# Gated delta rule: the state-free part of all chunks computed beside convolution and memory projection and kept in DRAM, on one Trainium2 core

## The chip, the cores and the metric

The kernel runs on one core of a Trainium2 chip. The metric is the device time of one execution in microseconds, the median of several runs. Before the change it is 1636.0 us (three runs, 1629.88 to 1637.38).

## What is computed

One layer of a hybrid decoder trunk on x of 1024 positions by 1024 columns, all float32. Cut to what matters here:

```
h = rms_norm(x);  proj = h @ w_in
qkv, z, a, b, c_q, c_kv, k_idx, w_idx, ug = split(proj)
qkv = silu(causal_depthwise_conv(qkv, 4 taps))     # 4 heads of 128, for q, k and v
q, k = l2_norm(q), l2_norm(k)                      # per head and position
# delta rule in chunks, here of 128 positions, 8 chunks; gamma = decay inside a chunk
A  = strict_lower(beta k k^T * gamma);  qk = lower(q k^T * gamma)
u, w = solve(I + A, [beta v, beta k exp(decay)])
# scan over chunks with a state S (128x128 per head):
v_new = u - w S;  o = (q exp(decay)) S + qk v_new;  S = S exp(last) + k_dec^T v_new
y_a = rms_norm(o) * silu(z)
y_b = attention over the 256 best-scored earlier positions (top-k) of 4 heads of 64
y_c = silu(layer_norm(causal_depthwise_conv(u * sigmoid(gate), 31 taps)))
x += [y_a | y_b | y_c] @ w_out
x += cross_attention(rms_norm(x), rms_norm(mem))   # mem: 256 positions, wkv 1024x1024
x += relu(rms_norm(x) @ w1)^2 @ w2
```

Of the delta rule, A, qk, the decays, beta v and k_dec do not depend on S; they are called the state-free part here. The inverse of I + A does not either, and is built in two steps: exact inverses of its 16x16 diagonal blocks, then doubling.

## The kernel before

A full-precision product is three matmuls on split operands (high x high, low x high, high x low; helper `mm3`, L133 to L135), and splits are made by `unit` (L171 to L185; high part on ACT or POOL, low part on POOL or DVE). The program is written as Python generators that yield an estimated cost; `weave` interleaves several of them in proportion to given rates, `some` takes a part of one, and each engine executes its own instructions in the order so produced. SP issues nearly all DMAs, in order as well. `psum(3)` divides the eight PSUM banks into three for the delta rule ("mg") and five for the rest ("mm").

The stages around the change, in time order (the stretches are those of the rows below):

- **164 to 318 us and 318 to 458 us.** `qkv_stage` (L722): 12 column blocks, each two halves of 24 matmuls of 512 columns; ACT copies the result out (L733), makes two of the four taps (L738), POOL and DVE (L741) add the others, ACT applies Silu (L743), and the block goes to `qkv_d` in DRAM. Beside it `topk` (L559) searches the threshold of six score blocks bit by bit, 33 steps: in each, ACT counts four blocks (L588), DVE two, and DVE then moves the candidate (L597). Beside both, `conv_taps` (L773): the 31-tap convolution as 62 steps of six matmuls with diagonal weights; POOL makes a pair of diagonal tiles (L784) for every four steps, two pairs at a time. Then `z_gate` (8 groups of 24 matmuls), the memory's norm (`mem_norm`), and `gdn_norms` (L747): q and k are loaded again, turned by 64 PE transposes (L759) and squared and summed by ACT (L761).
- **458 to 548 us.** State-free part of chunks 0 and 1 (`gdn_pre`, L890), block inverses of chunk 0 (`gdn_blocks`, L961: one chunk on 32 partitions, loaded from and stored to DRAM), doubling of chunk 0 (`gdn_post`, L1002), beside the memory projection (`mem_stage`), the end of `topk`, and `conv_norm`.
- **548 to 772 us.** Nine rounds n: `gdn_scan` of chunk n-1, `gdn_post` of n, `gdn_blocks` of n+1, `gdn_pre` of n+2, and a share (11.0) of `dsa_out`, which is the selected attention and the w_out product.
- From 772 us cross attention and the MLP follow; neither is touched.

In the loop of `run` the rates are:

```
ths.append((self.gdn_scan(gpb, n - 1, c[n - 1]), 6.0))
ths.append((self.gdn_post(gpc, n, c[n]), 8.0))
ths.append((self.gdn_blocks(gpa, n + 1), 4.0))
ths.append((self.gdn_pre(gpa, n + 2, c[n + 2]), 5.0))
ths.append((self.some(fill, 11.0, True), 11.0))
```

Of the kernel before, what the change touches and what calls it, by code (L numbers as in the profile page):

```python
# [20 lines left out]
F32 = mybir.dt.float32  # L21
# [11 lines left out]
P = 128  # L33
T = 1024
# [16 lines left out]
class Block:  # L51
# [155 lines left out]
    def mem_norm(self, wu, mp, yp):  # L207
# [12 lines left out]
        self.mT = [mp.tile([P, KT, 256], F32R, name=f"mT{i}", tag=f"Y{i}") for i in range(2)]  # L220
# [15 lines left out]
    def mem_stage(self, wu, mp):  # L236
# [322 lines left out]
    def topk(self, pool, SC, HI, LO, NEGM):  # L559
# [60 lines left out]
        EQ = NEGM  # L620
        for j, b in enumerate(order):
            K = (b + 1) * P

            V.tensor_scalar(EQ[b], SC[b], TH[:, j:j + 1], None, op0=OP.is_equal, op1=OP.add, accum_out=neq[:, j:j + 1])
            if b in acts:
                Sc.activation(junka[:, :K], SC[b], AF.Sign, bias=TH[:, j:j + 1], scale=-1.0, accum_out=nsg[:, j:j + 1])
            else:
                V.tensor_scalar(junk[:, :K].bitcast(BF), SC[b], TH[:, j:j + 1], None, op0=OP.is_gt, op1=OP.add,
                                accum_out=nsg[:, j:j + 1])

        na = len(acts)
        V.tensor_add(r[:, :na], nsg[:, :na], neq[:, :na])
        for j, b in enumerate(acts):
            V.memset(thr[:, j:j + 1], 256.0 - (b + 1) * 64)
        V.scalar_tensor_tensor(r[:, :na], r[:, :na], 0.5, thr[:, :na], op0=OP.mult, op1=OP.add)
        V.tensor_scalar(r[:, na:], nsg[:, na:], -1.0, 256.0, op0=OP.mult, op1=OP.add)
        for j, b in enumerate(order):
            K = (b + 1) * P
            cs = pool.tile([P, T], F32, name="cs", tag="kc", bufs=1)[:, :K]
            V.tensor_tensor_scan(cs, EQ[b], EQ[b], 0.0, op0=OP.add, op1=OP.bypass)  # L640

            V.scalar_tensor_tensor(cs, cs, r[:, j:j + 1], EQ[b], op0=OP.is_gt, op1=OP.mult)
# [104 lines left out]
    def gdn_norms(self, pool):  # L747
# [1061 lines left out]
```

## Time and profile before

| | |
|---|---|
| median of three runs | 1636.0 us (1629.88 to 1637.38) |
| the profiled execution's own time | 1631.19 us |
| its span, first to last instruction | 1629.4 us |
| busy over the span: PE, DVE, ACT, POOL | 1508.6, 1171.4, 739.6, 318.6 us |
| mean granted TensorE clock, share of full | 0.972 |
| stretches that the change touches | 164 to 772 us |

A busy time is the sum over an engine's instructions; matmuls are pipelined and their ends are modelled, so PE at 93% of the span still has room in places. The rows below give it by stretch: from:to, length, then busy time and number of instructions for PE, PEld, DVE, ACT and POOL, then the granted clock, the DMA engines' share and GB/s. The granted clock is the share of full speed that TensorE had. In rows of waits, "PE a <- POOL b: total, times, longest" is the time in which PE stood before a and POOL's b ended last.

### The profile page before, as it was taken

The numbers are of one execution on the slowest core, as the hardware profiler recorded it, in microseconds if no ns is written. First come the engines' busy times: TensorE is split into PE (matmuls) and PEld (weight loads), VectorE is DVE, ScalarE is ACT, GpSimd is POOL, SyncE is SP. The second block draws the span as 40 slices with busy tenths as digits, with TensorE's granted clock in tenths as the row PEclk, the third lists the DMA queues.
The fourth block names the chain that finished last, engine by engine and source line by source line (L and its number), as shares of the span: only waits on it lengthen the run. The fifth ranks groups of instructions, "written<-read, shape, count | busy, mean of one in ns | idle before, by whom it ended". The sixth has DMA issues, their size and how long they took to land.

```text
span 1629.4 us, 20582 instructions
## 1 busy us (share of the span) xinstructions
PE 1508.6 (93%) x7497; PEld 1256.2 (77%) x7497; DVE 1171.4 (72%) x2149; ACT 739.6 (45%) x1483; POOL 318.6 (20%) x297
## 2 busy tenths in 40 slices
PE   6999999997975789999979996999999999999999
PEld 6877788885775678888768875888888888888887
DVE  7649868678258688985767777996569656865783
ACT  4535777883541656665434542433224223323331
POOL 3021434345355333221401103100000000000000
PEclk9999999998997999999999997999999999999999
DMA  6130121221543533323712356813551364146202
GB/s 213 38 97 21 45 59 52 78 67 44 163 152 98 168 115 119 94 59 128 289 66 75 120 186 265 330 57 130 206 208 34 134 235 165 52 155 242 95 7 97
DMA packets 113811, 201.93 MB, mean 124 GB/s; under 512 B 15157, under 2 KB 64046, under 8 KB 106542
## 3 DMA queue, kind: packets, MB, share of 16 engines
q1 hardware_dynamic: 112174, 195.37, 34.8%
q0 software_dynamic: 1536, 5.24, 0.9%
q8 instruction: 59, 0.97, 0.2%
q14 instruction: 42, 0.34, 0.1%
HBM read 150.26 MB, written 50.33 MB: 123 GB/s over the span
## 4 chain that ended last, share of the span: by engine, by line
PE 65%; DVE 16%; ACT 9%; issue 5%; DMA 3%; POOL 1%; SPq 0%; ACTq 0%; DVEq 0%; POOLq 0%
PE mlp_mm L134 13%; PE mlp_mm L135 13%; PE mlp_mm L133 13%; ACT junka L588 5%; DVE acc L741 1%; PE gi_mm L1029 1%; PE xq_mm L133 1%; PE xq_mm L134 1%; PE xw_mm L135 1%; PE xw_mm L133 1%; PE xw_mm L134 1%; PE xq_mm L135 1%; DVE tk_t L596 1%; PE small_mm L135 1%; DVE junk L590 1%
## 5 line engine op out<-in xcount | busy, mean ns | idle before, releaser
L134 PE MATMUL mlp_mm<-bm,wm 128*128 128x512 f32 x448 | 178.6, 399 | 11.9 <-DVE bm L1456 11.9
L133 PE MATMUL mlp_mm<-bm,wm 128*128 128x512 f32 x448 | 178.0, 399 | 2.5 <-DVE rs_x L156 1.3
L135 PE MATMUL mlp_mm<-bm,wm 128*128 128x512 f32 x448 | 178.1, 398 | 0.0
L135 PE MATMUL mlp_mm<-wm,am 128*128 128x512 f32 x448 | 177.1, 395 | 0.0
L134 PE MATMUL mlp_mm<-wm,am 128*128 128x512 f32 x448 | 177.0, 395 | 0.0
L133 PE MATMUL mlp_mm<-wm,am 128*128 128x512 f32 x448 | 175.1, 395 | 0.0
L1455 ACT CAST wm<-wq 128x2048 fp32r<-128x2048 f32 x32 | 61.2, 1911 | 211.9 <-PE mlp_mm L134 211.7
L1545 DVE TENSOR_TENSOR xacc<-xacc,mlp_mm 128x512 f32<-128x512 f32 x112 | 75.9, 684 | 69.7 <-PE mlp_mm L135 69.7
L134 PEld LDWEIGHTS mlp_mm<-bm,wm 128*128 128x128 f32 x448 | 85.0, 190 | 33.0 <-DVE bm L1456 12.7
L133 PEld LDWEIGHTS mlp_mm<-bm,wm 128*128 128x128 f32 x448 | 85.1, 190 | 23.4 <-DVE rs_x L156 1.6
L135 PEld LDWEIGHTS mlp_mm<-bm,wm 128*128 128x128 f32 x448 | 85.1, 190 | 20.3
L133 PEld LDWEIGHTS mlp_mm<-wm,am 128*128 128x128 f32 x448 | 84.1, 188 | 20.4
L134 PEld LDWEIGHTS mlp_mm<-wm,am 128*128 128x128 f32 x448 | 84.1, 188 | 20.4
L135 PEld LDWEIGHTS mlp_mm<-wm,am 128*128 128x128 f32 x448 | 84.1, 188 | 20.3
L1456 DVE TENSOR_TENSOR wm<-wq,wm 128x2048 fp32r<-128x2048 f32 x32 | 73.3, 2291 | 28.6 <-ACT wm L1455 28.3
L1455 ACT CAST wm<-wsum 128x2048 fp32r<-128x2048 f32 x24 | 45.9, 1912 | 105.5 <-PE mlp_mm L134 79.3
L1456 DVE TENSOR_TENSOR wm<-wsum,wm 128x2048 fp32r<-128x2048 f32 x24 | 54.9, 2289 | 51.5 <-ACT wm L1455 51.5
L1509 ACT ACTIVATE aq<-mlp_mm 128x512 f32<-128x512 f32 x64 | 38.1, 595 | 72.8 <-PE mlp_mm L135 72.7
L185 POOL TENSOR_TENSOR wlo<-wraw,whi 128x1024 fp32r<-128x1024 f32 x28 | 68.5, 2445 | 1.7
L133 PE MATMUL cv_mm<-Y,diag 128*128 128x512 f32 x124 | 50.2, 405 | 11.2 <-POOL diag L784 11.2
L588 ACT ACTIVATE junka<-negm,tk_cand 128x384 bf16<-128x384 int16 (+1 forms) x68 | 52.6, 774 | 16.4 <-DVE tk_cand L597 13.7
L588 ACT ACTIVATE junka<-lo,tk_cand 128x384 bf16<-128x384 uint16 (+1 forms) x64 | 49.5, 773 | 18.5 <-DVE tk_cand L597 12.5
(515 smaller groups left out, 4092.7 us busy)
## 6 DMA issues: line engine op xcount, KB each, us to landing
bm<-hb_d SPq DMA_DIRECT2D x42, 1024.0 KB, 4.9
wq<-in_mlp_w SPq DMA_DIRECT2D x32, 1024.0 KB, 5.3
hb_d<-bm SPq DMA_DIRECT2D x14, 1024.0 KB, 4.0
wraw<-in_w_in SPq DMA_DIRECT2D x20, 512.0 KB, 4.0
qkv_d<-acc SPq DMA_DIRECT2D x12, 512.0 KB, 3.2
x<-in_x SPq DMA_DIRECT2D x8, 512.0 KB, 4.2
gnx<-qkv_d SPq DMA_DIRECT2D x8, 512.0 KB, 6.3
wraw<-in_xa_wkv SPq DMA_DIRECT2D x8, 512.0 KB, 6.0
```

The costliest lines, as they stand in the source:

```text
L133: mm(out, l[0], r[0], start=start, stop=False, skip_group_check=on)
L134: mm(out, l[0], r[1], start=False, stop=False, skip_group_check=on)
L135: mm(out, l[1], r[0], start=False, stop=stop, skip_group_check=on)
L185: (lo_eng or nc.gpsimd).tensor_sub(lo[:, :n], raw[:, :n], hi[:, :n].bitcast(F32))
L588: Sc.activation(junka[:, :K], X[b], AF.Sign, bias=c, scale=-1.0, accum_out=n)
L590: V.tensor_scalar(junk[:, :K].bitcast(X[b].dtype), X[b], c, None, op0=OP.is_lt, op1=OP.add, accum_out=n)
L596: V.tensor_tensor(t, cnt, th, op=OP.is_le)
L741: nc.vector.scalar_tensor_tensor(acc, xb[:, 3 - d:3 - d + T], self.cw[:, 3 - d, i:i + 1], acc, op0=OP.mult, op1=OP.add)
L1455: Sc.copy(w[0], x)
L1456: V.tensor_sub(w[1], x, w[0].bitcast(F32))
L1509: Sc.activation(x, ps[ch, m], AF.Relu if c == "21" else AF.Copy)
L1545: V.tensor_add(x, x, ps[ch, tt])
```

## The change

1. **First stretch.** `psum(3)` is called ahead of it. `qkv_stage` and `z_gate` run in sequence beside all 33 search steps, but with only 18 of the 62 convolution steps, which start late. `gdn_norms` no longer loads and turns q and k: inside `qkv_stage`, ACT squares each of the eight q and k blocks at once (128x1024), and 64 one-column matmuls against a vector of ones, two blocks later, give the sums.
2. **Middle stretch.** The state-free part of all eight chunks, in pairs, with the block inverses of four chunks at once on 128 partitions (same instructions, 128 instead of 32 partitions, two calls instead of eight); beside it `mem_norm` and `mem_stage`, the end of `topk` and the other 44 convolution steps with `conv_norm`. Five results per chunk (vb, kd, qE, qkT, NAT, 256 KB each) are stored to `gp_d` in DRAM, by SP. The wkv splits go to ACT (high) and alternately POOL and DVE (low). In `topk`'s end ACT takes the sign of all six blocks, POOL compares and makes the mask, DVE scans.
3. **Last stretch.** Eight rounds of scan, post of the next chunk, a share of 12.4 of `dsa_out`, and loads of the kept tiles.

```
-        ss = C.tile([P, NT, 2 * H], F32, name="qkss")
-        for n in range(NT):
-            x = pool.tile([P, 2 * H, P], F32, name="gnx", bufs=2)
-            nc.sync.dma_start(x, self.qkv_d[n, :, 0:2 * H, :])
...
+            for n in range(NT):
+                nc.tensor.matmul(ps[:, n:n + 1], sq[i][:, n * P:(n + 1) * P], self.one, start=True, stop=True)
+            nc.vector.tensor_copy(self.qkss[:, :, i], ps)
...
+            if i < 2 * H:
+                sq[i] = wp.tile([P, T], F32, name="sq", bufs=2)
+                nc.scalar.activation(sq[i], acc, AF.Square)
+            if 0 <= i - 2 < 2 * H:
+                sums(i - 2)
...
-        N = H * 8
+        N = 4 * H * 8
         A, W = (pool.tile([N, 272], F32, name=x, bufs=1) for x in ("Ab", "Wb"))
-        nc.sync.dma_start(A[:, 0:256], self.Ab_d[n].rearrange("b j i -> b (j i)"))
+        nc.sync.dma_start(A[:, 0:256], self.Ab_d[n:n + 4].rearrange("n b j i -> (n b) (j i)"))
...
+    def gdn_keep(self, n, i, t):
+        self.nc.sync.dma_start(self.gp_d[n, i], t.rearrange("p h c -> p (h c)"))
...
-        NB = 3
+        NB = 2
...
-            qkv = self.qkv_stage(wu, wp, hT)
-            self.drain(self.weave((self.seq(self.some(qkv, 18), self.some(mem, 2), qkv), 5.2), (self.some(topk, 28), 1.15),
-                                  (self.some(conv, 54), 3.0)))
+            self.drain(self.weave((self.seq(self.qkv_stage(wu, wp, hT), self.z_gate(wu, zp, hT)), 5.2),
+                                  (self.some(topk, 33), 1.05), (self.seq(iter([17.0]), self.some(conv, 18)), 1.33)))
...
-        self.drain(self.weave((pre, 1.0), (self.mem_stage(wu, mkp), 2.6), (topk, 0.7), (self.conv_norm(cva, myp), 0.7)))
+        pre = [both(0, 1), both(2, 3), self.weave((both(4, 5), 1.0), (self.gdn_blocks(gpa, 0), 0.4)),
+               self.weave((both(6, 7), 1.0), (first(0), 0.6)), self.gdn_blocks(gpa, 4)]
+        self.drain(self.weave((self.seq(*pre), 4.4), (self.seq(self.mem_norm(wu, mtp), self.mem_stage(wu, mkp)), 2.6),
+                              (topk, 1.0), (self.seq(conv, self.conv_norm(cva)), 6.0)))
...
+            for n in range(NT):
+                ths = [(self.gdn_scan(gpb, n, c[n]), 6.0)]
+                if n + 1 < NT:
+                    self.gdn_load(gpl, n + 1, c[n + 1])
+                    ths.append((self.gdn_post(gpc, n + 1, c[n + 1]), 8.0))
+                if n + 2 < NT:
+                    self.gdn_load_A(gpc, n + 2, c[n + 2])
+                ths.append((self.some(fill, 12.4, True), 12.4))
```

How the order moves, at three places (line numbers after the change are up to 20 higher).

ACT in the first stretch. junka is a search count's discarded output, xb a column block of qkv, acc and xtap its taps. Before:

```order
L738 ACTIVATE acc<-xb,taps 128x1024
L738 ACTIVATE xtap<-xb,taps 128x1024
L588 ACTIVATE junka,tk_cnt<-negm_95,tk_cand 128x768
L588 ACTIVATE junka,tk_cnt<-negm_92,tk_cand 128x384
L588 ACTIVATE junka,tk_cnt<-negm_93,tk_cand 128x512
L588 ACTIVATE junka,tk_cnt<-negm_94,tk_cand 128x640
L588 ACTIVATE junka,tk_cnt<-negm_95,tk_cand 128x768
L733 COPY xb<-qkv_mm 128x512
L743 ACTIVATE acc<-acc 128x1024
L588 ACTIVATE junka,tk_cnt<-negm_92,tk_cand 128x384
```

and after:

```order
L745 ACTIVATE acc<-xb,taps 128x1024
L745 ACTIVATE xtap<-xb,taps 128x1024
L592 ACTIVATE junka,tk_cnt<-negm_95,tk_cand 128x768
L592 ACTIVATE junka,tk_cnt<-negm_92,tk_cand 128x384
L592 ACTIVATE junka,tk_cnt<-negm_93,tk_cand 128x512
L592 ACTIVATE junka,tk_cnt<-negm_94,tk_cand 128x640
L740 COPY xb<-qkv_mm 128x512
L592 ACTIVATE junka,tk_cnt<-negm_95,tk_cand 128x768
L750 ACTIVATE acc<-acc 128x1024
L592 ACTIVATE junka,tk_cnt<-negm_92,tk_cand 128x384
L755 ACTIVATE sq<-acc 128x1024
```

The counts of the search stand among the copies and taps as before, two search steps to a column block, and the eight squares (sq) are new.

POOL in the middle stretch. negm is the mask tile that the end of the search writes, cs the scan's result on DVE, diag the diagonal weights of the next four convolution steps; gsq, qE and qkT belong to the state-free part. Before, where convolution and the search's end met:

```order
L784 AFFINE_SELECT diag<-dwh 128x512
L784 AFFINE_SELECT diag<-dwl 128x512
L739 TENSOR_TENSOR acc<-acc,xtap 128x1024
L644 TENSOR_SCALAR negm_92<-cs 128x384
L644 TENSOR_SCALAR negm_93<-cs 128x512
L184 TENSOR_SCALAR whi<-wraw 128x1024
L185 TENSOR_TENSOR wlo<-wraw,whi 128x1024
L784 AFFINE_SELECT diag<-dwh 128x512
L784 AFFINE_SELECT diag<-dwl 128x512
```

and after:

```order
L641 TENSOR_SCALAR negm_95<-cs 128x768
L964 AFFINE_SELECT qkT<-E 128x512
L185 TENSOR_TENSOR wlo<-wraw,whi 128x1024
L641 TENSOR_SCALAR negm_96<-cs 128x896
L964 AFFINE_SELECT qkT<-E 128x512
L955 TENSOR_TENSOR gsq<-NAT,bm 128x512
L785 AFFINE_SELECT diag<-dwh 128x512
L785 AFFINE_SELECT diag<-dwl 128x512
L976 TENSOR_TENSOR qE<-qE,ed 128x512
L955 TENSOR_TENSOR gsq<-NAT,bm 128x512
L641 TENSOR_SCALAR negm_97<-cs 128x1024
L976 TENSOR_TENSOR qE<-qE,ed 128x512
```

The diagonal pairs, which had stood among splits and taps, stand there behind masks, which wait for DVE, and behind steps of the state-free part.

SP where the last stretch begins. KA, VS and QAb are the operands of the selected attention, Wb the block inverses. Before:

```order
L257 DMA kT_d<-kvt_4546 128x512
L1000 DMA Xb_d<-Wb 32x256
L257 DMA kT_d<-kvt_4547 128x512
L1014 DMA xc<-Xb_d 128x4x16
L1644 DMA KA_4668<-KA_d 128x1024
L1644 DMA KA_4669<-KA_d 128x1024
L1645 DMA VS<-VS_d 128x1024
L1113 DMA QAb<-QA_d 128x512 x2
```

and after:

```order
L905 DMA lNAT<-gp_d 128x512
L1034 DMA xc<-Xb_d 128x4x16
L1020 DMA Xb_d<-Wb 128x256
L1669 DMA KA_5116<-KA_d 128x1024
L1669 DMA KA_5117<-KA_d 128x1024
L1670 DMA VS<-VS_d 128x1024
L899 DMA lvb<-gp_d 128x512
L899 DMA lkd<-gp_d 128x512
L899 DMA lqE<-gp_d 128x512
L899 DMA lqkT<-gp_d 128x512
L901 DMA lkT<-qkv_d 128x512
L899 DMA lvb<-gp_d 128x512
```

The store of the second four chunks' block inverses now stands right ahead of KA, and ten loads of kept tiles stand ahead of QAb.

## Rows read from the trace of the kernel before

**Rows 1.** Windows: busy time of PE, PEld, DVE, ACT, POOL, the four stretches.

```profile
164.00:318.00 154.00, 153.18 (x659) 123.73 (x658) 112.81 (x218) 118.95 (x241) 62.88 (x56) 1.00 0.21 62
318.00:458.00 140.00, 126.14 (x565) 102.64 (x564) 83.17 (x136) 79.84 (x250) 60.51 (x47) 0.94 0.29 90
458.00:548.00 90.00, 57.87 (x390) 52.56 (x389) 63.53 (x154) 25.50 (x67) 49.30 (x52) 0.87 0.46 147
548.00:772.00 224.00, 202.17 (x1451) 181.94 (x1449) 182.78 (x580) 139.59 (x360) 59.13 (x67) 0.99 0.33 101
```

**Rows 2.** Windows, 40 us of the MLP, with 128x512 matmuls on PE.

```profile
1080.00:1120.00 40.00, 40.00 (x173) 32.20 (x172) 34.41 (x28) 13.17 (x7) 0.00 (x0) 1.00 0.16 53
```

**Rows 3.** Timeline of PE at 36 us: start, length, instruction.

```profile
36.20 1.03 PE L203 MATMUL n_mm<-ident,n_y 128*128 128x128 f32 x8
37.07 0.60 PE L350 MATMUL small_mm<-ident,sm 128*128 128x128 f32 x4
```

**Rows 4.** Groups of ACT, 164 to 318 us: busy, mean ns, then idle before.

```profile
L588 ACT ACTIVATE junka<-negm,tk_cand 128x384 bf16<-128x384 int16 (+1 forms) x68 | 52.6, 774 | 16.4 <-DVE tk_cand L597 13.7 <-DVE negm L556 1.3
L738 ACT ACTIVATE xtap<-xb,taps 128x1024 f32<-128x1024 f32 x8 | 9.1, 1139 | 0.0
L733 ACT COPY xb<-qkv_mm 128x512 f32<-128x512 f32 x16 | 9.0, 565 | 0.0
L743 ACT ACTIVATE acc<-acc 128x1024 f32<-128x1024 f32 x7 | 7.4, 1059 | 4.7 <-DVE acc L741 4.7
```

**Rows 5.** Timeline of ACT, the first counts of two search steps on end.

```profile
177.35 0.62 ACT L588 ACTIVATE junka<-negm,tk_cand 128x384 bf16<-128x384 int16 x1 [0.50 <-DVE tk_cand L597]
181.41 0.61 ACT L588 ACTIVATE junka<-negm,tk_cand 128x384 bf16<-128x384 int16 x1 [0.49 <-DVE tk_cand L597]
```

**Rows 6.** Groups of ACT, 424 to 454 us.

```profile
L761 ACT ACTIVATE gn_mm<-gn_mm 128x128 f32<-128x128 f32 x59 | 15.4, 261 | 0.9 <-PE gn_mm L759 0.8
```

**Rows 7.** Groups of DVE, 458 to 772 us, in gdn_pre.

```profile
L930 DVE SCALAR_TENSOR_TENSOR G<-gp_mm,rg_y,E 128x128 f32<-128x128 f32 x32 | 9.3, 340 | 3.0 <-ACT E L917 1.8 <-PE gp_mm L927 1.2
L950 DVE SCALAR_TENSOR_TENSOR qkT<-gp_mm,rg_y,qkT 128x128 f32<-128x128 f32 x32 | 9.3, 339 | 1.6 <-PE gp_mm L948 1.6
L939 DVE TENSOR_REDUCE dc<-gsq 128x64 f32<-128x512 f32 x8 | 8.2, 1030 | 0.0
L932 DVE TENSOR_TENSOR NAT<-gp_mm,G 128x512 f32<-128x512 f32 x8 | 5.4, 680 | 0.0
```

**Rows 8.** Windows of tile Tb alone, DVE: all of gdn_blocks.

```profile
458.00:772.00 314.00, 61.02 (x144) 0.96 0.36 114
548.00:772.00 224.00, 43.00 (x108) 0.99 0.33 101
```

**Rows 9.** Windows of tile cs alone, DVE then POOL.

```profile
300.00:458.00 158.00, 26.01 (x18) 5.63 (x6) 0.95 0.30 91
```

**Rows 10.** Groups of POOL, 318 to 458 us: the masks of the search's end.

```profile
L644 POOL TENSOR_SCALAR negm<-cs 128x384 bf16<-128x384 f32 (+5 forms) x6 | 5.6, 938 | 19.6 <-DVE cs L643 19.5
```

**Rows 11.** Waits of PE, 164 to 458 us.

```profile
PE cv_mm L133 <- POOL diag L784: 11.2, 2, 10.4
```

**Rows 12.** Timeline at 498 us, POOL and DVE.

```profile
498.23 4.68 POOL L835 TENSOR_TENSOR cyc<-cyc,conv_ln_b 128x1024 f32<-128x1024 f32 x2
498.40 2.19 DVE L157 TENSOR_SCALAR rs_i<-rs_x 128x4 int32<-128x4 int32 x1
```

**Rows 13.** Timeline of SP, and of PE at the first matmul on KA.

```profile
486.80 0.33 SPq L968 DMA_DIRECT2D Ab<-Ab_d  x1
...
516.83 0.32 SPq L1000 DMA_DIRECT2D Xb_d<-Wb  x1
...
537.27 0.97 SPq L1644 DMA_DIRECT2D KA<-KA_d  x2
...
544.70 0.33 PE L1122 MATMUL da_mm<-KA,QAb 128*128 128x128 f32 x1 [0.91 <-DMA QAb<-QA_d]
```

**Rows 14.** DMA issues by line: count, KB, median us to landing.

```profile
Ab<-Ab_d SPq DMA_DIRECT2D x8, 32.0 KB, 1.6
```

More of the change, by code (lines that the diff above doesn't have):

```diff
@@ L219, in mem_norm @@
         self.stage = "mem"
-        self.mT = [mp.tile([P, KT, 256], F32R, name=f"mT{i}", tag=f"Y{i}") for i in range(2)]
+        self.mT = [mp.tile([P, KT, 256], F32R, name=f"mT{i}") for i in range(2)]
         for g in range(4):
@@ L619, in topk @@
         TH = ih.bitcast(F32)
-        EQ = NEGM
+        yield 0.5
+        half = pool.tile([P, N], F32, name="tk_half")
+        for j, b in enumerate(order):
+            V.memset(half[:, j:j + 1], 256.0 - (b + 1) * 64)
         for j, b in enumerate(order):
             K = (b + 1) * P
[L624 to L638, printed above, removed]
[L639 to L644 removed]
+            sg = LO[b].bitcast(BF)
@@ L645, in topk @@
+            V.scalar_tensor_tensor(cs, cs, r[:, j:j + 1], sg, op0=OP.is_gt, op1=OP.add)
+            nc.gpsimd.tensor_scalar(NEGM[b], cs, 0.0, NEG, op0=OP.is_gt, op1=OP.mult)
             yield 1.0
@@ L1616, in run @@
-        with sb_pool(tc, "gnp", bufs=1, side="right") as gnp:
-            self.drain(self.weave((self.seq(self.some(z, 3), mem, self.weave((z, 5.2), (self.gdn_norms(gnp), 2.0))), 5.2),
-                                  (self.some(topk, 7), 1.0), (conv, 5.0)))
-        self.psum(3)
-        mkp = ts.enter_context(sb_pool(tc, "mkp", bufs=1, side="right"))
+            self.drain(self.weave((self.seq(self.qkv_stage(wu, wp, hT), self.z_gate(wu, zp, hT)), 5.2),
+                                  (self.some(topk, 33), 1.05), (self.seq(iter([17.0]), self.some(conv, 18)), 1.33)))
@@ new lines, in run, with both, first @@
+        gpa = cvs.enter_context(sb_pool(tc, "gdna", bufs=1))
+        mtp = cvs.enter_context(sb_pool(tc, "mtp", bufs=1))
+        mkp = cvs.enter_context(sb_pool(tc, "mkp", bufs=1))
+        self.block_mask(gpc)
+        def both(a, b):
+            return self.weave((self.gdn_pre(gpa, a), 1.0), (self.gdn_pre(gpa, b), 1.0))
+        def first(n):
+            self.gdn_load_A(gpc, n, c[n])
+            yield from self.gdn_post(gpc, n, c[n])
+        pre = [both(0, 1), both(2, 3), self.weave((both(4, 5), 1.0), (self.gdn_blocks(gpa, 0), 0.4)),
+               self.weave((both(6, 7), 1.0), (first(0), 0.6)), self.gdn_blocks(gpa, 4)]
```

103 lines of the change are left out of this document (54 added, 49 removed).

## The prediction

> **What bounds the kernel now.** I read the windows by stretch first. The change touches only 164 to 772 us, 608 us of the span, and the rest I leave as it is. In the windows [rows 1] the reader is to see that the stretches differ. From 164 to 318 us PE is busy 153.2 of 154 us. From 318 to 458 it is busy 126 of 140, from 458 to 548 only 58 of 90, and from 548 to 772 it is busy 202 of 224 beside a DVE with 183. A busy PE is not PE at its peak, so I price its work by what passes when it runs alone: 173 matmuls of 512 columns in 40 us [rows 2], 0.231 us each, and eight of 128 columns between 36.20 and 37.07 us [rows 3], 0.109 us each. For 256 columns I take half of the first, 0.116 us.
>
> With these prices and the program's counts the stretch 548 to 772 us holds 1451 matmuls: 240 of 512 columns (55.4 us), 16 of 384 (some 2.8), 160 of 256 (18.6) and 1035 of 128 (112.8), together 190 us in 224 us. So the loop runs at 1.18 times PE's full pace, and 34 us of it are waits. The stretches from 318 to 548 us hold about 162 us of such work in 230 us. The change can gain the loss in these places and nothing from the matmuls themselves, most of which stay.
>
> **First stretch.** PE keeps 576 matmuls of qkv (133.1 us) and 192 of z (44.4), takes 108 of the convolution's 372 (24.9), and 64 one-column ones, for which no row exists: above nothing and at most a 128-column one, 7 us; I take the upper end, since each loads its own weights. That is 209 us, of which qkv's part has 153 and z's 56. Beside qkv ACT now has 26 of the 33 search steps. A step takes 4.06 us from first count to first count, of which 0.49 is the wait for DVE's candidate (starts at 177.35 and 181.41 us; the mean count is 774 ns) [rows 4, 5]; 3.57 us of work times 26 is 92.8 us. With it go 24 copies at 0.565 (13.6 us), 22 taps at 1.14 (25.1) and, at a tap's price, 11 Silu and 8 new squares of the same shape (21.7) [rows 4]. That is 153 us. Nine step ends have nothing to cover their wait (9 x 0.49 = 4.4 us), and Silu's waits for the tap sums, 4.7 us for 7 blocks [rows 4], make 8 for 12. ACT needs 166 us where PE needs 153, so ACT sets the end: 166 + 56 = **222 us**. At best PE's 209; at worst ACT idles as much as from 164 to 318 us, 35 us [rows 1], which gives 153 + 35 + 56 = 244. The removed norm stage takes 64 small squares at 261 ns (16.7 us) from ACT [rows 6] and 64 transposes (7 us) from PE; both are already absent from the sums.
>
> **Middle stretch.** PE has 264 convolution matmuls (61.0 us), 192 of the memory projection at 0.116 (22.3), 256 in the state-free part of eight chunks (27.9), 60 for chunk 0's doubling (6.5) and 40 transposes (4.4): 122 us. DVE's work: 63.5 us from 458 to 548 [rows 1], where the program has the state-free part of three chunks and two block inverses, as many calls as now; five more chunks at 32.2/8 us (9.3 + 9.3 + 8.2 + 5.4) [rows 7] add 20.1; one block inverse is 61.0/8 = 7.6 us [rows 8], and I take the same price for four chunks on four times the partitions, because the elements per partition stay. The search's end adds about 18, two of the three operations behind 26.0 us [rows 9]. That makes 102. POOL has 49.3 [rows 1] and about 30 more operations (diagonals and masks) of the size of a mask, 0.938 us [rows 10], with the splits that leave it set against the products of five more chunks: 77. PE is still the longest, so waits decide. I take the loop's ratio, because the work is of that kind, chains of small operations beside long matmuls: 122 x 1.18 = **144 us**. The ends are 122 and 179. The upper one is DVE and POOL in turn; it also takes in a few waits like the 10.4 us one, in which a convolution matmul stood before its diagonal tile [rows 11].
>
> At 498 us a DVE operation on 128x4 elements lasted 2.19 us while POOL ran two additions in 4.68 us [rows 12], yet from 548 to 772 us the two sum to 242 us in 224 [rows 1], so they overlap there at least by 18 us. The Trainium skill ("SBUF — State Buffer", Who interferes with whom) has the two share a port pair as an exclusive lock, for DVE operations with two SBUF inputs or in a two-port mode against GpSimd reads: by that rule the sum would hold the upper end 179, by the loop's row 144. The first row agrees with it; the loop's sum shows that not every pair of operations locks.
>
> **Boundary.** The second call of the block inverses stands last, its store right ahead of KA on SP, and ten loads of kept tiles ahead of QAb. DVE's 7.6 us [rows 8], from KA's issue at 537.27 to the first matmul at 544.70 us another 7.4 [rows 13], and three small transfers at 1.6 us [rows 14] make 20; behind the last pair PE has about 80 small matmuls left (9 us), so I charge **12 us**. Below: 7.4, all else covered. Above: before, the elapsed time from the load to the store was 30 us [rows 13], so 30 + 7.4 - 9 = 28. The 40 stores of 256 KB and 48 loads go on the same SP queue; each costs SP about 0.33 us [rows 13], 29 us over some 350, so I charge nothing beyond this place. The Trainium skill ("Perfetto Trace Analysis", DMA Optimizations) advises one issuing engine for inputs and another for outputs where there are loops; by that rule the upper end, 28, is the value, and no run here shows it.
>
> **Last stretch.** Of the loop's 190 us of PE work, the five state-free parts in it go, 160 matmuls (17 us): 173. DVE loses 43.0 us [rows 8] and 20 of the state-free part [rows 7], and falls from 183 to 120. Then DVE is no longer close behind PE, and I keep half of the 34 us of waits: **190 us**. The ends are 173 and 173 x 1.18 = 204.
>
> **Sum.** 222 + 144 + 12 + 190 = 568 us against 608: 40 us less. The profiled execution took 1631.19 us (span 1629.4), 0.3% under the median of 1636.0, so the forecast is **1591 us**. About 0.5%, 8 us, is what a measurement of this kernel can tell from no change.
>
> **Rivals.**
> - *PE alone decides.* If ACT's waits vanish under PE and the loop's waits go with DVE's load: 209 + 122 + 12 + 173 = 516, so 1539 us. For it: PE was at 153 of 154 us beside the same search and taps [rows 1]. Against: there, other matmuls were at hand. Chance 0.10.
> - *POOL's order (slower than before).* In the middle nine pairs of diagonal tiles stand on POOL behind masks and state-free products. Masks had waited 19.6 us for DVE [rows 10], and then PE stood 10.4 us [rows 11]. If all nine pairs are late by as much, 94 us go, 22 of which are in the ratio: 568 + 72 = 640, so 1663 us. It decides against the change above an average of (40 + 8 + 5 + 22)/9, about 8 us a pair (5 us from the profiled execution to the median). Against: two pairs are kept ahead, 11 us of matmuls. Chance 0.10.
> - *DVE and POOL take turns*, as [rows 12], throughout the middle: 102 + 77 = 179 in place of 144, so 1626 us, hardly a gain. Chance 0.11.
> - *The boundary is long*: 28 in place of 12, so 1607 us, when the block inverse again takes 30 us between its load and its store. Chance 0.13.
>
> **How the numbers follow.** The forecast itself gets 0.54, with a range of its own of 1570 to 1615; 0.02 are left for what I don't see. Range: 1552 to 1632 leaves out POOL's order (0.10), half of PE alone (0.05) and a little of the upper side (0.03). Faster by over 0.5% (under 1628): the forecast, PE alone, the boundary and half of the turns, less a little for the unknown, 0.80. Within 0.5%: the other half and the edge, 0.09. Slower: POOL's order and the edge, 0.11.
>
> **What would show it.** Right: qkv ends 166 us after 164 with ACT the busier (over 0.9) and PE under 0.95 there; the middle about 144 us long, its PE waits spread over many small ones; one wait of 5 to 15 us at the first matmul on KA; DVE near 120 us in the last stretch of about 190. Wrong: a PE busy throughout the first stretch (PE alone), waits on diagonals above 5 us each (POOL's order), DVE operations of over 2 us beside POOL in numbers (turns).

## The result, and the profile after

The changed kernel took 1611.76 us (median of 4 runs, 1610.89 to 1615.11) against 1635.35 us of the kernel before on the same chip; the ratio is 0.9865 with a 95% interval of 0.9842 to 0.9889. It is faster by 23.6 us where 44 were forecast. The profiled execution took 1610.89 us, 20.3 less than the one of before; its span is 1609.2 us.

The stretches of the profile after, in the same view as [rows 1] (from:to, length, busy time and instructions of PE, PEld, DVE, ACT, POOL, then granted clock, DMA share, GB/s): qkv, z, the front of the middle stretch up to the first state-free matmul, the rest of its state-free part, the boundary up to the first attention matmul, and the last stretch.

```profile
164.50:333.70 169.20, 167.32 (x772) 137.61 (x771) 128.12 (x225) 132.83 (x258) 74.67 (x56) 0.98 0.24 69
333.70:389.30 55.60, 54.88 (x236) 44.14 (x235) 38.34 (x78) 44.28 (x96) 24.29 (x19) 1.00 0.25 74
389.30:420.50 31.20, 21.97 (x86) 16.44 (x84) 15.49 (x38) 10.19 (x19) 29.39 (x31) 0.84 0.30 96
420.50:529.90 109.40, 105.44 (x696) 94.40 (x696) 69.79 (x158) 49.54 (x133) 61.12 (x52) 0.98 0.59 191
529.90:553.40 23.50, 10.15 (x55) 8.00 (x53) 18.84 (x50) 3.90 (x8) 7.63 (x4) 0.69 0.93 325
553.40:756.90 203.50, 188.91 (x1317) 170.79 (x1318) 135.45 (x429) 121.04 (x295) 41.23 (x47) 0.97 0.50 161
```

| stretch | forecast | measured |
|---|---|---|
| first (164.5 to 389.3 us) | 222 | 224.8 |
| middle (to 540.2, PE's last transpose there) | 144 | 150.9 |
| boundary (to 553.4) | 12 | 13.2 |
| last (to 756.9) | 190 | 203.5 |
| sum | 568 | 592.4 |

The same ends of before, 164.8 to 774.0 us, are 609.2 us apart, so these stretches gave 16.8 of the 40 us forecast for them. Cross attention, with the rest of the w_out product, took 203.3 us against 200.8, though 16 matmuls more of that product (some 4 us) now lie in the last stretch. The MLP, up to the end, took 649.0 against 654.6, though its code is the same. From its first matmul to its last it took 649 to 652 us in the profiles of four kernels of this study (the one before, and b_noblocks, e3_late and x_no_mem of the next section) and 643 to 646 in the other fourteen. PE's waits for DVE's part of a split operand (bm) go with it. They are, in us in total, times and longest, before:

```profile
PE mlp_mm L134 <- DVE bm L1456: 11.9, 2, 8.7
```

and after:

```profile
PE mlp_mm L134 <- DVE bm L1476: 8.0, 2, 4.8
```

The longest is 8.6 to 9.0 us in those four and 4.3 to 4.8 in the others; what sets it is not known. So some 6 us of the gain are not explained by the change, and below, runs are also compared by the time from the first qkv matmul to the first MLP matmul in their profiles, called S: 810.0 us before, 795.7 after, 796.3 in a second profile of the changed kernel.

What the reader should see in the rows: PE is idle 3 us in qkv and z, then 9 us of the 31 at the front and 13 of the 24 at the boundary. At the boundary the granted clock falls to the lower level (0.50), and the DMA engines are busy nearly all the time:

```profile
530.00:540.00 10.00, 4.80 (x33) 3.51 (x31) 9.35 (x27) 2.16 (x6) 2.08 (x2) 0.93 0.80 255
540.00:550.00 10.00, 3.13 (x14) 2.53 (x12) 8.27 (x22) 0.10 (x1) 2.04 (x1) 0.50 1.01 372
550.00:560.00 10.00, 5.53 (x21) 4.59 (x22) 6.47 (x20) 5.52 (x14) 4.62 (x5) 0.50 0.86 294
560.00:570.00 10.00, 7.63 (x47) 7.02 (x47) 6.94 (x22) 8.75 (x18) 4.14 (x5) 0.70 1.03 374
```

### The profile page after: what moved, and what is told of

It reads as the page before. It is cut to its first block, busy times and chain, and to the rows that moved or that the text cites. A ratio compares the mean times of both kernels' runs of the same rounds, so it can differ in the third digit from the quotient of the medians.

```text
span 1609.2 us, 20703 instructions
## 1 busy us (share of the span) xinstructions
PE 1513.7 (94%) x7561; PEld 1261.1 (78%) x7561; DVE 1136.0 (71%) x2042; ACT 736.2 (46%) x1375; POOL 326.7 (20%) x279
## 4 chain that ended last, share of the span: by engine, by line
PE 65%; DVE 14%; ACT 9%; issue 5%; DMA 4%; POOL 3%; SPq 0%; ACTq 0%; POOLq 0%; DVEq 0%
PE mlp_mm L134 13%; PE mlp_mm L135 13%; PE mlp_mm L133 13%; ACT junka L592 4%; DVE acc L748 1%; PE xq_mm L133 1%; PE wa_mm L135 1%; PE wa_mm L133 1%; PE wa_mm L134 1%; PE xw_mm L135 1%; PE xw_mm L133 1%; PE xw_mm L134 1%; PE xq_mm L134 1%; PE xq_mm L135 1%; DVE junk L594 1%
## 5 line engine op out<-in xcount | busy, mean ns | idle before, releaser
L135 PEld LDWEIGHTS mlp_mm<-bm,wm 128*128 128x128 f32 x448 | 85.0, 190 | 20.3
L1476 DVE TENSOR_TENSOR wm<-wsum,wm 128x2048 fp32r<-128x2048 f32 x24 | 59.3, 2472 | 51.3 <-ACT wm L1475 51.3
L133 PE MATMUL qkv_mm<-hT,whi 128*128 128x512 f32 x192 | 77.7, 404 | 0.9 <-ACT xb L740 0.9
L134 PE MATMUL qkv_mm<-hT,whi 128*128 128x512 f32 x192 | 76.7, 399 | 0.0
L135 PE MATMUL qkv_mm<-hT,wlo 128*128 128x512 f32 x192 | 76.7, 399 | 0.0
L185 POOL TENSOR_TENSOR wlo<-wraw,whi 128x1024 fp32r<-128x1024 f32 x24 | 57.9, 2412 | 3.4 <-issue 1.9
```

What stands on the lines that cost most here:

```text
L133: mm(out, l[0], r[0], start=start, stop=False, skip_group_check=on)
L134: mm(out, l[0], r[1], start=False, stop=False, skip_group_check=on)
L135: mm(out, l[1], r[0], start=False, stop=stop, skip_group_check=on)
L185: (lo_eng or nc.gpsimd).tensor_sub(lo[:, :n], raw[:, :n], hi[:, :n].bitcast(F32))
L1476: V.tensor_sub(w[1], x, w[0].bitcast(F32))
```

## The experiments

Every run is of one edit or a few; ratios are to the kernel before, medians of the runs. The changed kernel again, on the chip of x_12, e8_gz_pool and x_gz:

> The changed kernel once more, on the same chip as the three below, as their measure: 1608 to 1616 us, from the start of qkv to the start of the MLP 794 to 797 us, first state-free matmul some 31 us behind z's last.

Measured: 1610.75 us, ratio 0.9861 (0.9836 to 0.9887), S 796.3. The first result stands.

### What the parts are worth

**b_norms: the norms' new form alone, in the kernel before** (their squares with one buffer, for room, and the sums one block behind instead of two):

```
+                sq[i] = wp.tile([P, T], F32, name="sq", bufs=1)
+                nc.scalar.activation(sq[i], acc, AF.Square)
...
-            self.drain(self.weave((self.seq(self.some(z, 3), mem, self.weave((z, 5.2), (self.gdn_norms(gnp), 2.0))), 5.2),
+            self.drain(self.weave((self.seq(self.some(z, 3), mem, z), 5.2),
```

> One part of the change alone, in the kernel before: q's and k's norms from eight squares and 64 one-column sums in the qkv stage, no second load and no turning of q and k. Theory (a sum is two instructions of 0.112 us, so PE takes on 14.3 us where it is never idle, and gives back 64 transposes at 0.109 and the waits around them, 10.8 us): no gain, -3 to +4 us on the kernel before. Rival (ACT's 64 small squares with their reads, 28 us, set the end of that stretch): 8 to 15 us faster.

Measured: 1639.04 us, ratio 1.0036 (1.0019 to 1.0053), S 823.0. The norms' new form is a small loss, 5.7 us, a little beyond the theory's 4, and ACT's squares were hidden. Up to the first state-free matmul it costs nothing, as the theory has it: that matmul comes 298.2 us behind the first of qkv, and came 297.5 behind it before. The rest of what S lost lies behind it and is not explained. What the sums cost is in PE's groups of the changed kernel, out and in, count, busy and mean ns:

```profile
L731 PE MATMUL qkv_mm<-one,sq 128*128 128x1 f32 x128 | 15.4, 250 | 1.0 <-DVE qkss L732 1.0
```

A one-column product of float32 is two instructions, 128 for 64. They follow one another every 0.112 us, about as 128-column ones do (0.109 [rows 3]), 14.3 us in all. The prediction had 64 and called 7 us the upper end.

**a_blocks1: block inverses of one chunk per call again** (with the loads and stores to fit):

```
-        N = 4 * H * 8
+        N = H * 8
...
-               self.weave((both(6, 7), 1.0), (first(0), 0.6)), self.gdn_blocks(gpa, 4)]
+               self.weave((both(6, 7), 1.0), (first(0), 0.6)), self.seq(*(self.gdn_blocks(gpa, i) for i in range(4, 8)))]
```

> The changed kernel with the block inverses of one chunk per call again, eight calls on 32 partitions in place of two on 128: 46 us more on DVE, all in the middle and at the boundary. Theory (the seam's last four calls stand alone between the last pair and the stores, and DVE has 95 us of work in 151 us there): 20 to 35 us slower than the changed kernel, about the time of the kernel before. Rival (DVE's load is hidden beside PE, as the 128 partitions save nothing on the path): within 5 us of the changed kernel.

Measured: 1650.78 us, ratio 1.0109 (1.0085 to 1.0134), 39 us more than the changed kernel and more than the 20 to 35 expected, S 833.5. Without the 128 partitions the change is slower than the kernel before: of the 38 us in S, 24 lie between the last state-free and the first scan matmul (41 us in place of 17). No run moves the state-free part alone, so what that is worth by itself is not shown. In the changed kernel the two calls cost DVE 14.6 us, 7.3 a call, where one chunk's call had cost 7.6 [rows 8], in the windows of tile Tb alone:

```profile
389.00:540.00 151.00, 14.58 (x36) 0.95 0.55 175
```

**b_noblocks: the kernel before without the inverses in its loop** (it leaves out those of chunks 1 to 7; every chunk uses chunk 0's):

```
-                if n + 1 < NT:
-                    ths.append((self.gdn_blocks(gpa, n + 1), 4.0))
...
-        nc.sync.dma_start(xc[:, :, 0, :], self.blk_view(self.Xb_d, n))
+        nc.sync.dma_start(xc[:, :, 0, :], self.blk_view(self.Xb_d, 0))
```

> The kernel before without the block inverses of chunks 1 to 7 (every chunk uses those of chunk 0): some 53 us less of DVE work in the stretches from 458 us, 43 of them in the loop. Rival (the prediction's step: DVE, 183 us of 224, makes half of the loop's waits): the loop, 229 us from the first attention matmul to the last of the scan, shortens by 12 us or more. Theory (PE's order and the chains of post and scan make the waits, DVE's load does not): it shortens by less than 5 us.

Measured: 1613.38 us, ratio 0.9891 (0.9861 to 0.9922). From the first attention matmul to the scan's last it took 213.4 us in place of 229.3:

```profile
546.70:760.10 213.40, 201.41 (x1481) 184.80 (x1482) 152.23 (x485) 142.25 (x369) 57.95 (x62) 1.00 0.35 108
```

PE is idle 12 us there, against 23 in the loop of before (229.3 us with 206.3 busy), and its 1481 instructions are busy 4.8 us less. DVE is busy 152.2 us there in place of 185.5. So this expectation's theory fell, and the prediction's step held: it took half of 34 us, 17, for what DVE's load costs the loop, and the inverses alone, 33 us of that load, cost it 15.9.

### The front of the middle stretch

**e1_sums_r: the sums in the split format** (F32R, the type of the split operands), one instruction each (the squares sq are of it too):

```
-                nc.tensor.matmul(ps[:, n:n + 1], sq[i][:, n * P:(n + 1) * P], self.one, start=True, stop=True)
+                nc.tensor.matmul(ps[:, 2 * n:2 * n + 2], sq[i][:, n * P:(n + 1) * P], self.oner, start=True, stop=True)
```

> The changed kernel's 64 one-column sums are done in the split format (one instruction of PE each in place of two), into two columns each. In the trace of the changed kernel they are 128 instructions of 0.112 us, 14.3 us. Theory (PE paces the qkv part: 162 of its 168 us are PE's own pace): 5 to 7 us less than the changed kernel's 1611.8, so about 1606. Rival (ACT sets the end there, as the prediction had it): no difference, 1610 to 1614.

Measured: 1611.28 us, ratio 0.9882 (0.9846 to 0.9917), S 796.6. Both were half right. From first to last the qkv part shortened by 7.6 us (161.6 for 169.2), so PE paces it and not ACT; yet the time did not move. The first state-free matmul comes at 417.1 us, 34.5 behind z in place of 31.2, and from there to the MLP it takes 5.8 us longer.

**e2_iseq_dve: the comparisons on DVE:**

```
-            nc.gpsimd.tensor_scalar(NEGM[b], sg, 0.0, 0.0, op0=OP.is_equal, op1=OP.add)
+            V.tensor_scalar(NEGM[b], sg, 0.0, 0.0, op0=OP.is_equal, op1=OP.add)
```

> The comparisons at the end of the search (L633) go from POOL to DVE; all else as in the changed kernel. Theory (five of them, 14.8 us on POOL from 385 to 402 us, hold the diagonal tiles behind them, and PE works 5 of 17 us there): 6 to 10 us less, 1602 to 1606. Rival (the load and norm of mem, or the wkv splits, set that stretch): within 2 us of 1611.8.

Measured: 1611.79 us, ratio 0.9880 (0.9843 to 0.9916), S 789.9. S gained the 6 us that were expected at least, the median none: the profiled execution, 1606.43 us, was the fastest of the four by 4.7, and its S speaks for it alone. What the comparisons hold is in the changed kernel's timeline of POOL (start, us, instruction, in brackets the idle time before it):

```profile
384.01 11.65 POOL L633 TENSOR_SCALAR negm<-lo 128x384 bf16<-128x384 bf16 x5 [0.85 <-ACT lo L632]
...
397.33 4.61 POOL L633 TENSOR_SCALAR negm<-lo 128x1024 bf16<-128x1024 bf16 x1
401.93 1.36 POOL L669 TENSOR_SCALAR zt<-zt,taps 128x512 f32<-128x512 f32 x2
...
409.59 0.69 POOL L669 TENSOR_SCALAR zt<-zt,taps 128x512 f32<-128x512 f32 x1
```

and in that of SP, its queue's transfers:

```profile
402.64 0.36 SPq L670 DMA_DIRECT2D gz_d<-zt  x1
403.40 0.37 SPq L180 DMA_DIRECT2D wraw<-in_xa_wkv  x1
403.86 0.49 SPq L670 DMA_DIRECT2D gz_d<-zt  x1
414.96 0.37 SPq L180 DMA_DIRECT2D wraw<-in_xa_wkv  x1
415.43 0.46 SPq L670 DMA_DIRECT2D gz_d<-zt  x1
415.94 0.49 SPq L920 DMA_DIRECT2D Lk<-qkv_d  x1
416.49 0.49 SPq L920 DMA_DIRECT2D Lv<-qkv_d  x1
```

Six comparisons take 16.4 us on POOL (six on DVE: 0.26 to 0.67 us each). Behind them on POOL wait z's gates (zt), and behind each gate SP's store of it (gz_d). The last gate is done at 410.3 us; its store and, from 415.9 us, the loads of the first pair (Lk, Lv) then stand behind a load of wkv's weights (wraw), which waits for DVE's low split of those before (wlo). As the timelines have it, that split too is late by way of the comparisons. DVE's scan (cs) waits for the mask that stands behind five of them on POOL, mem's norm follows the scan on DVE, and ACT's last step of it (whi) follows that, until 403.4 us; behind this step come SP's next load of wkv's weights, PE's transposes and ACT's high splits. In DVE's timeline:

```profile
397.28 1.23 DVE L635 TENSOR_TENSOR_SCAN cs<-negm 128x512 f32<-128x512 bf16 x1 [5.56 <-POOL negm L641]
...
411.71 3.23 DVE L185 TENSOR_TENSOR wlo<-wraw,whi 128x1024 fp32r<-128x1024 f32 x1 [0.46 <-ACT whi L182]
```

and in ACT's:

```profile
402.22 1.15 ACT L219 ACTIVATE whi<-wraw,mem_y 128x1024 f32<-128x1024 f32 x1 [7.74 <-DVE mem_y L168]
```

With the comparisons gone (e2) the loads are issued at 408.5 us, and yet the first state-free matmul comes at 420.7: ahead of it PE first waits 4.8 us, until 407.4, for mem's norm. So SP's order is one of several links, and an edit changes which of them ends last.

**x_12: both together, nothing else:**

> The sums in the split format and the comparisons on DVE, nothing else. Theory (PE and POOL are both late at the front of the middle, each hides the other): the first state-free matmul at 405 to 409 us as in the run with three edits, against 420.5, and 10 to 14 us off the changed kernel's time. Rival (the third edit, the later loads at the boundary, is needed): under 6 us off.

Measured: 1594.49 us (1592.07 to 1598.13), ratio 0.9762 (0.9737 to 0.9786), 16.3 us under the changed kernel on the same chip; S 778.8. The theory holds: each alone left the median where it was (1611.28 and 1611.79 us), both together take 16 off; in S it is +0.9, -5.8 and -17. The first loads are issued at 402.9 us, behind a load of wkv's weights that waited for mem's norm until 401.9:

```profile
382.96 0.36 SPq L672 DMA_DIRECT2D gz_d<-zt  x1
...
391.77 0.36 SPq L672 DMA_DIRECT2D gz_d<-zt  x1
401.88 0.37 SPq L182 DMA_DIRECT2D wraw<-in_xa_wkv  x1
402.35 0.46 SPq L672 DMA_DIRECT2D gz_d<-zt  x1
402.86 0.49 SPq L922 DMA_DIRECT2D Lk<-qkv_d  x1
403.40 0.48 SPq L922 DMA_DIRECT2D Lv<-qkv_d  x1
```

Of the 17 us, 8.2 are in qkv and z, 4.8 between z and the first state-free matmul (26.4 for 31.2); the rest is spread. Why the sums alone lost 6 us behind the front is not settled.

**e6_mem_rows: mem's norm between qkv and z**, with the convolution's outputs as its memory:

```
-            y = wu.tile([P, D], F32R, name="whi", bufs=2).bitcast(F32)
+            y = mp.tile([P, D], F32, name=f"my{t}", tag=f"cacc{t}")
...
-            self.drain(self.weave((self.seq(self.qkv_stage(wu, wp, hT), self.z_gate(wu, zp, hT)), 5.2),
+            self.drain(self.weave((self.seq(self.qkv_stage(wu, wp, hT), self.mem_rows(wu, cva, ys), self.z_gate(wu, zp, hT)), 5.2),
```

> The squares, roots and scalings of mem's norm run between qkv and z again, into the memory of the convolution's outputs; its transposes stay in the middle. Theory (the middle's front, 393 to 410 us, where PE does 16 transposes, is mem's norm behind the search's end on DVE and ACT): the transposes no longer wait, the middle shortens by 5 to 12 us; from the start of qkv to the start of the MLP 784 to 791 us in place of 795.7. Rival (SP holds the state-free part's first loads until 416 us behind the stores of z's gate, which wait for POOL): the first state-free matmul stays at about 420 us and the gain is under 3 us.

Measured: 1634.60 us, ratio 1.0001 (0.9980 to 1.0022), S 819.8: a miss of both. The front did not shorten (first state-free matmul at 424.3 us), and the boundary grew to 36 us from the last state-free matmul to the first of the scan, in place of 17, as told below.

**x_all and x_no_mem: e1, e2 and e3 (later loads of the kept tiles, below) together, with e6 and without:**

> Four edits together: the sums in the split format, the search's comparisons on DVE, mem's norm between qkv and z, the kept tiles' loads in the course of a round. Theory (the qkv part is paced by PE, and each further saving is lost at the front of the middle as long as one of POOL, DVE and SP is late there): 7.6 us of the sums and 5 to 12 of the front and 2 of the boundary now show together; from the start of qkv to the start of the MLP 775 to 783 us, the time about 1595. Rival (the search's own chain of ACT and DVE ends at 383 us whatever PE does, and the middle follows it): 786 to 792.

> As x_all, but mem's norm stays in the middle stretch, as in the changed kernel. Theory (the front of the middle is late on several engines at once, and mem's norm is one of them): from the start of qkv to the start of the MLP 787 to 792 us, between the changed kernel's 795.7 and x_all's 782.1. Rival (mem's norm was harmless, its move alone cost 22 us through the order at the boundary): 778 to 783.

Measured: x_all 1595.55 us, 0.9770 (0.9742 to 0.9797), S 782.1; x_no_mem 1602.27 us, 0.9805 (0.9777 to 0.9834), S 780.3. The rival of the second holds in S: moving mem's norm is worth nothing; part of the 7 us in the medians is the MLP, 652.2 us in the profile without it and 645.8 with it. Neither beats x_12, so no gain of the later loads shows there either.

**e8_gz_pool and x_gz: the gate's stores on POOL's queue**, alone and with x_all:

```
-                nc.sync.dma_start(self.gz_d[n * 4:n * 4 + 4, :, h, :].rearrange("t p c -> p t c"),
+                nc.gpsimd.dma_start(self.gz_d[n * 4:n * 4 + 4, :, h, :].rearrange("t p c -> p t c"),
```

> The changed kernel with the stores of z's gate issued by POOL, which makes the gate, in place of SP. Theory (SP's order is the link: its loads of the first pair's tiles stand at 415.9 us behind a store that waits for POOL): the first state-free matmul comes 8 to 15 us earlier, near 408, and 4 to 10 us go off the time. Rival (the first state-free step waits for the memory of z's tiles and of hT, or PE is held by mem's transposes in any case): first state-free matmul within 3 us of 420, time within 2 us.

> All four edits of x_all and the gate's stores on POOL. Theory (SP's order is still a link there, its first load at 401 us): 2 to 6 us less than x_all's 1595.5. Rival (once POOL is free at 400 us the stores no longer wait): within 2 us of x_all.

Measured: 1635.69 us, 1.0008 (0.9992 to 1.0025), S 816.9; and 1617.43 us, 0.9914 (0.9886 to 0.9942), S 794.3. Both slower, which neither expected. In the first the loads of the pair are issued at 417.2 us, behind loads of wkv's weights that wait for mem's norm (until 399.5) and then for the splits of those before (until 416.7), and the first state-free matmul comes at 432.2, later than the rival had it. So SP's order is a link, but not through this store alone; and the boundary is long again.

### The boundary

**e3_late: the kept tiles' loads in the course of a round** (`late` issues them after 7.0 of a round's cost):

```
-                    self.gdn_load(gpl, n + 1, c[n + 1])
+                    ths.append((late(n + 1), 12.4))
```

> The five kept tiles of the next chunk are loaded in the course of a round instead of at its start, so that five loads less stand on SP ahead of QAb at the boundary. Theory (the ten loads at 540 to 547 us, with the DMA engines busy all the time, delay the first attention matmul): the first matmul on KA 2 to 4 us earlier and as much off the time, 1608 to 1610. Rival (the banks of PSUM that DVE empties at 546.6 us gate PE, the loads are hidden behind that): within 1 us of 1611.8.

Measured: 1612.19 us, ratio 0.9891 (0.9855 to 0.9928), S 793.9. The first attention matmul came 2.9 us behind the scan's first in place of 6.4; the time did not change, as the rival has it.

**e4_conv8: the convolution earlier:**

```
-                              (topk, 1.0), (self.seq(conv, self.conv_norm(cva)), 6.0)))
+                              (topk, 1.0), (self.seq(conv, self.conv_norm(cva)), 8.0)))
```

> The convolution's rate in the middle goes from 6.0 to 8.0, so that its norm comes ahead of the second block inverses and the memory projection ends last. Theory (PE's idle 6.7 us at 540 to 547 is the wait for DVE's end of the convolution's norm): that wait goes and 3 to 7 us with it, 1605 to 1609. Rival (whatever stands last takes its place, the block inverse or the projection's norm): 1610 to 1616.

Measured: 1615.57 us, ratio 0.9903 (0.9869 to 0.9938), S 802.4. The rival: the memory projection's transposes now end at 542 us, and the scan begins at 552.2.

**e5_keep_busy: PE kept busy** by 130 transposes:

```
+        pd = self.mm_ps([P, 512])
+        for i in range(130):
+            nc.tensor.transpose(pd[:, 0:P], self.ident, self.ident)
```

> 130 transposes of the identity (14 us of PE) are added where the middle stretch ends, so that PE is not idle from 530 to 547 us; they compute nothing. Theory (part of what was lost at the start of the last stretch is PE at its lower clock, granted 0.50 from 540 to 560 and 0.70 to 570 us): the granted clock stays 1.00 to 547 us, and PE's work from 547 to 567 us, some 12 us at full pace, gains 3 to 6 us; from the start of qkv to the start of the MLP 790 to 793 us in place of 795.7. Rival (PE waits there for data, its clock is of no account): 795 to 798.

Measured: 1615.52 us, ratio 0.9902 (0.9870 to 0.9934), S 799.7. The granted clock stays up at first and falls later:

```profile
529.00:553.50 24.50, 20.63 (x177) 20.21 (x176) 18.28 (x49) 2.31 (x6) 3.67 (x3) 0.95 0.90 314
553.50:573.00 19.50, 10.41 (x54) 9.17 (x52) 12.59 (x41) 12.75 (x29) 9.93 (x8) 0.62 0.74 239
```

The scan's first matmul came 4 us later than in the changed kernel (551.1 for 547.0 us), behind the transposes, the first attention matmul at the same time (553.5). From there to 573 us PE still waits for data, and its clock is 0.62. So no gain of a higher clock was to be had in this way; what the lower clock costs by itself stays open, since it fell again in the wait that follows.

**x_ka_act: KA and VS loaded by ACT, in x_all:**

```
-                nc.sync.dma_start(KA[i].bitcast(F32), self.KA_d[i])
-            nc.sync.dma_start(VS.bitcast(F32), self.VS_d)
+                nc.scalar.dma_start(KA[i].bitcast(F32), self.KA_d[i])
+            nc.scalar.dma_start(VS.bitcast(F32), self.VS_d)
```

> As x_all, with the loads of KA and VS issued by ACT in place of SP, so that they don't stand behind the store of the last block inverses and its waits. Theory (the boundary is SP's order): the first attention matmul comes 3 to 6 us earlier after the last state-free one and as much goes off the time, 1590 to 1593. Rival (the DMA engines, busy all the time from 523 to 550 us in x_all, or PSUM's banks gate it): within 2 us of x_all.

Measured: 1595.59 us, 0.9772 (0.9750 to 0.9793). The rival holds: the first attention matmul comes 18.3 us behind the last state-free one, for 19.8 in x_all, so the queue is at most a small part of what gates KA.

How the boundary grows from 17 us to 35 is seen in e8's profile, in SP's timeline:

```profile
553.26 0.37 SPq L840 DMA_DIRECT2D yc_d<-cyc  x1
...
556.70 0.39 SPq L840 DMA_DIRECT2D yc_d<-cyc  x1
558.55 0.33 SPq L1020 DMA_DIRECT2D Xb_d<-Wb  x1
...
561.98 0.90 SPq L1669 DMA_DIRECT2D KA<-KA_d  x2
```

and in the changed kernel's timeline of SP:

```profile
537.55 0.32 SPq L1020 DMA_DIRECT2D Xb_d<-Wb  x1
537.92 0.92 SPq L1669 DMA_DIRECT2D KA<-KA_d  x2
...
554.58 0.37 SPq L840 DMA_DIRECT2D yc_d<-cyc  x1
...
556.86 0.37 SPq L840 DMA_DIRECT2D yc_d<-cyc  x1
```

The edits at the front change the order at the boundary too. In the changed kernel DVE ends the last block inverses before the convolution's norm, and KA's load is issued at 537.9 us, 8 behind the last state-free matmul. In e8 the steps of the norm come in between; the inverses' store (Xb_d) follows at 558.6 us behind the norm's first stores (yc_d), and KA's load at 562, 27 behind. In e6 the order of the stores is the same, with the inverses' at 550.1 and KA at 553.9, 28 behind. In x_gz the inverses' store stands first, and yet it is the same cause. Its last state-free matmul ends at 514.3 us; DVE does steps of the norm (cyc) from 522.5 to 528.8 amid the inverses and ends these at 533.6. SP waits 15 us for that, and KA's load is issued at 536.6, 22 behind:

```profile
533.61 0.32 SPq L1025 DMA_DIRECT2D Xb_d<-Wb  x1
...
536.60 1.51 SPq L1675 DMA_DIRECT2D KA<-KA_d  x2
```

The scan's tiles are loaded behind KA, and PE, which ran its last matmul ahead of the scan at 518.8 us, waits for one of them until 548.3:

```profile
PE gs_mm L1093 <- DMA lvb<-gp_d: 29.5, 1, 29.5
```

## Why the prediction was right and wrong

- **Direction, and the part that carries it: right.** The block inverses on 128 partitions cost what they cost on 32, and without them the change loses 39 us and is slower than before.
- **First stretch, 222 us: right in size, wrong in reason.** "ACT needs 166 us where PE needs 153, so ACT sets the end" failed. PE had 167.3 of 169.2 us, ACT 132.8. On PE's side the term that was mis-sized is the sums, 14.3 us in place of 7. The marks named for it were a PE under 0.95 and ACT over 0.9; PE was at 0.99, ACT at 0.79. So the size is luck: an ACT time that was too long stood for a PE time that was too short.
- **Middle, 144 us, measured 150.9: low.** That is 1.24 times the 122 us of PE's work, where 1.18 was taken, and the loss is not spread as that ratio has it: PE is idle 9 of the 31 us at the front, 4 of the 109 behind it and 5 of the last 10. The sum of POOL, 77 us where 92.7 were measured, left out the comparisons, 16.4 us, which its "about 30 more operations" did not have. It also took the masks at the price of before, 0.938 us each, where they were another operation: six now took 15.4 us (last section). z's gates and mem's norm wait behind the comparisons; with them on DVE and the sums shorter (x_12), the front took 26.4 us. The waits of the rival "POOL's order" did not come: no wait on a diagonal tile is among PE's longest there, and the longest of all is 3.0 us. DVE had 94.7 us and POOL 92.7 in 150.9, so they overlapped by 36 us at least; six DVE operations took over 2 us, five of them on 896 or 1024 columns: no turns "in numbers".
- **Boundary, 12 us, measured 13.2: right in size, but not by its chain.** It was priced as one wait, for the inverses and KA. PE's longest wait there is that of the scan's first matmul, and what ended last before it, by the profile, was a step of the convolution's norm on DVE (cyc), which the sum did not have:

```profile
PE gs_mm L1088 <- DVE cyc L834: 6.7, 1, 6.7
```

  PE was already half idle from 530 us, and the clock was at its lower level (0.50) from 540 to 560 us, with the DMA engines at 1.01 and 0.86.
- **Last stretch, 190 us, measured 203.5: the largest miss, and the step that failed.** The prediction kept "half of the 34 us of waits" for the whole stretch, and of the loads it said "so I charge nothing beyond this place", with SP's 0.33 us each as their price. Half was about right where the loop runs: b_noblocks shows 15.9 of the 17 us, and behind its first 20 us the changed stretch has half of before's idle time on PE. At its start nothing was saved. Before:

```profile
544.70:564.00 19.30, 14.45 (x102) 12.91 (x103) 15.33 (x55) 14.74 (x46) 7.80 (x9) 0.91 0.32 105
564.00:774.00 210.00, 191.81 (x1381) 172.87 (x1381) 170.17 (x539) 128.74 (x324) 54.12 (x63) 1.00 0.34 104
```

  and after:

```profile
553.40:573.00 19.60, 13.80 (x79) 12.34 (x80) 15.09 (x53) 15.53 (x42) 5.37 (x8) 0.68 0.92 319
573.00:756.90 183.90, 175.11 (x1239) 158.45 (x1239) 120.36 (x377) 105.50 (x253) 35.86 (x39) 1.00 0.46 144
```

  Of the first 20 us PE is idle 5.8 after and was idle 4.9 before; of the rest 8.8 and 18.2. In the start PE passes 79 matmuls where it passed 102, with the DMA engines busy 0.92 of the time (0.32 before) and a granted clock of 0.68 (0.91). By the prediction's own prices these 79 are 8.8 us of work (an estimate), so the start has 10.8 us beyond PE's work, where half of before's 8 would be 4. That is some 7 of the 13.5 us missed; 4 more are the w_out matmuls that moved in, which no term had. In e8 and a_blocks1, which enter the stretch late, with the clock at 0.94 and 1.00 and the DMA engines at 0.68 and 0.72 in its first 20 us, it takes 192.2 and 190.6 us, with 36 and 42 matmuls fewer in it (6 and 7 us at those prices). How much of the start is waiting for data and how much the clock is not separated. DVE had 135 us in the stretch, not 120.
- **The rivals.** "The boundary is long" did not come in the changed kernel, where 17 us lie between the last state-free and the first scan matmul, but did in e6, e8 and x_gz (34 to 36 us). Its 1607 us are nearest to the result, by luck: the boundary took 13.2 us. "PE alone decides" holds in qkv and z.
- **A better kernel.** The changed one with both edits of x_12 reaches 1594.5 us, 3 us from the forecast. That is not the forecast's sum come true, as its last stretch takes 203.4 us too: its S is 31 us under before's, and most of the rest is again the MLP. The kernel as changed lost 16 us to the sums and the comparisons.

## What to carry to other kernels

A saving of waits that holds where a loop runs need not hold at its start: price the start by itself, and loads by how long the DMA engines take for them, not by what their issue costs. A step moved to a seam is to be followed through every in-order queue that it joins: here slow comparisons on POOL held z's gates and DVE's scans, the scans mem's norm, and gates and norm SP's stores and loads, and a saving on PE showed only when the comparisons were gone too. Where several engines are late at one seam, try the edits together before dropping one that did nothing alone.

## What the runs showed of the hardware that we had not expected

- A float32 matmul of one column is two instructions, each issued 0.112 us after the last, about as one of 128 columns is (0.109 [rows 3]); in the split format, two columns wide, it is one: 64 instead of 128, and 7.6 us less in the stretch.
- POOL's comparison of bf16 with a sum took 1.5 to 4.6 us on 384 to 1024 columns, DVE's 0.26 to 0.67 on the same. The masks of the changed kernel, which compare and multiply in one operation, took POOL 1.5 to 3.6 us; those of before, which multiply and add, took 0.5 to 1.8 on the same shapes and types, 0.94 in the mean [rows 10]. In the changed kernel's groups of POOL:

```profile
L641 POOL TENSOR_SCALAR negm<-cs 128x384 bf16<-128x384 f32 (+5 forms) x6 | 15.4, 2570 | 4.1 <-DVE cs L640 2.7 <-DVE rs_t L166 1.2
```

- In e6, a DVE product of 128x64 took 2.16 us, and another of the same line and shape 0.27 us five us later, in its timeline of DVE:

```profile
538.67 2.16 DVE L1019 TENSOR_TENSOR Tb<-Wb,Pb 128x64 f32<-128x64 f32 x1
...
543.45 0.27 DVE L1019 TENSOR_TENSOR Tb<-Wb,Pb 128x64 f32<-128x64 f32 x1
```

Beside the first, POOL added two tiles of 128x1024, in the same run's timeline of POOL:

```profile
537.45 5.59 POOL L839 TENSOR_TENSOR cyc<-cyc,conv_ln_b 128x1024 f32<-128x1024 f32 x2 [8.91 <-DVE cyc L838]
```

The Trainium skill ("SBUF — State Buffer", Who interferes with whom) has a DVE operation with two inputs in SBUF locked out by GpSimd reading there; these rows agree. The sum over a stretch is another matter: in the middle one the two overlapped by 36 us at least.
